# The pooling mixer as matrix products: group weights first, then band matrices, with the sums of the layer norm behind the last output tile

## The chip, the cores and the metric

The kernel runs on one core of a Trainium2 chip. A core has five engines that run side by side and are kept in step by semaphores: TensorE (PE in the profile, with its weight loads listed apart as PEld), VectorE (DVE), ScalarE (ACT), GpSimd (POOL) and SyncE (SP), which here only starts DMAs. The metric is the device time of one execution in microseconds; lower is better.

## What is computed

One inference step of a backbone with four layers, 1024 features and 384 tokens: a prompt of 128 and a sample of 256, which never mix. Each layer has a mixer and an MLP, and behind each of the two a residual and a layer norm. The mixers are, by layer: 0 an RG-LRU, 1 a short gated convolution, 2 a multi-scale pooling mixer, 3 an RG-LRU. The change concerns layer 2:

```python
WINDOWS = (2, 4, 8, 16)                       # one for each group of 256 features

def pool_mixer(x, w, scale):                  # x: tokens of one sequence
    S = cumsum of x over the tokens, with a zero in front
    for g, win in enumerate(WINDOWS):
        lo = clip(t - win // 2, 0, T)
        hi = clip(t + win - win // 2, 0, T)
        pooled[g] = (S[hi] - S[lo]) / (hi - lo)   # mean over a window, cut at the ends
    d = concat(pooled) - x
    y = d of group g times w[g]                   # 256 x 256 for each group
    return y * scale

x = layer_norm(ALPHA * x + g1 * out)
h = x * (1 + sc2) + sh2                       # the next input
```

Pooling works on the tokens alone and the group weights on the features alone, so the two can be done in either order.

## The kernel before

**Layout.** All activations lie transposed: eight tiles `Xt[c]` of 128 features (partitions) by 384 tokens (columns). A group of the pooling mixer is two tiles, `c = 2g` and `2g + 1`.

**Products in three parts.** Each float32 operand is split into a `hi` part, rounded to the type fp32r, and a `lo` part, the rest. A product is three TensorE instructions, hi·hi, lo·hi and hi·lo (`mm3`, lines 197 to 199 for the three). ScalarE writes the `hi` of weights (line 1289, `split_a`) and VectorE the `lo` (line 1295, `split_b`), 1024 columns at a time: half of a `raw` tile of 1 MB. The layer norm's sums are products with a matrix of 1/1024 (`ones_m`), in plain float32, which the profile lists as two records for each product.

**The order of the work.** `items` is a list of steps: `w` (half a weight tile, with a list of functions that are called one by one), `g` (a raw tile that is used as it is, mostly for the modulation vectors, `gemv`), `x` (a plain call) and `s` (a split). The loop at the end of the kernel runs through them. It calls `tick()` behind each function of a `w` item, and `defer(n, f)` runs `f` n ticks later. The splits of a weight half are deferred from three halves ahead (`LEAD`). Raw tiles have four buffers (`RAW_BUFS`) and are loaded by SyncE in the order of use as buffers come free (`issue`, line 1277). A scheduler then orders each engine's instructions: by the order of the program, but an instruction that is ready by its model may be put ahead of one that isn't. `tc.issue_after` holds instructions behind a given one on the same engine.

**Layer norm.** `ln_evac(idx)` gives a function `done(c, ps)` that adds an output tile to the residual (`resid`, line 547, two instructions, one for each sequence). From `c == 0` a mean over 128 features of the first tile is taken (`shift`, lines 567 and 568) and subtracted from all tiles (line 570). `stat(c)` squares a tile (line 582). Usually the sums over the tiles are kept on POOL or DVE (`s1t`, `s2t`, lines 594 to 598), and `stats_a` at the head of `ln_tail` makes four products of them (lines 619 to 622). With `late=True`, which only the pooling mixer uses, each tile and its square go to TensorE instead (line 588), one tile behind the outputs.

**The tail.** `tail` computes the variance `v` (line 648), its inverse root `r` (lines 649 to 655), and then, tile by tile in `chunk(c)`: subtract the mean (639), multiply by `r` (659), and `dst(c)`, the modulated `h` (705), its `hi` (718) and `lo` (723), and the next layer's `Xt[c]` (787 where the next norm is that of a mixer).

**The pooling mixer.** The tail ahead of it (`ln_tail(4, ..., lazy=True)`) leaves the tiles out; `pool_mix` calls `scaled(c)` and `pool_stage(c)` group by group from within the products (`before`). `lazy` also lets POOL subtract the mean for six tiles (line 647), and `kind == "pool"` lets ScalarE update `Xt[c]` (line 785). `pool_stage` works on DVE in a padded buffer of 392 or 408 columns: a shifted addition for windows 2 and 4 (lines 1113, 1116, 1117), a running sum and a difference for 8 and 16 (1119, 1122), a factor for the 8 columns at each end (1127), and the scaling and subtraction of `x` (1128). `new_h` then splits the result, with the `lo` part on POOL (line 723). Then come 16 products of 392 columns (`ORD_POOL`), two for each output tile.

**Around it.** `short_conv(1)` is layer 1's mixer; its first 32 weight tiles run with the input tiles outermost, so that TensorE can begin with the first tile of `h`. The tail ahead of it is `ln_tail(2, to_h(2, "mm"))`. `mlp(2)` follows the pooling mixer's own tail, `ln_tail(5)`.

## Time and profile before

| | |
|---|---|
| median of 3 runs | 1650.58 us (1650.07 to 1651.04) |
| profiled execution, its own time | 1649.62 us |
| its span, first to last instruction | 1647.8 us |
| mean granted TensorE clock | 0.989 |
| last product of layer 1's MLP starts | 881.29 us |
| variance (line 648) of the tail ahead of the pooling mixer | 884.36 us |
| first product of the pooling mixer | 898.68 us |
| variance (line 648) of the tail behind it | 931.80 us |
| first product of layer 2's MLP | 936.44 us |

Times inside the span are counted from its first instruction. A row of the timeline gives start, duration, engine, line, operation, output and inputs, and how many instructions of the kind were merged; a bracket gives the idle time ahead of it and what ended that. A row of the grouped lines gives the count, the total busy time and the mean in nanoseconds, and the idle time ahead of the group. A row of windows gives, for a stretch, its length, then the busy time and the number of instructions of PE, PEld, DVE, ACT and POOL, the granted clock, the busy share of the DMA engines and GB/s. TensorE instructions overlap, so their pace is read from one start to the next.

### The profile page before, as it was taken

The page shows a single profiled execution, that of the slowest core. Times are in us where ns is not written, and L with a number is a line of the kernel's source. Part 1 is how long each engine was busy: PE and PEld are TensorE (multiplying, and loading weights), DVE is VectorE, ACT ScalarE, POOL GpSimd, SP SyncE. Part 2 cuts the span into 40 slices and gives each one's busy share as a digit, 9 for nine tenths or more (in the row PEclk, how much of TensorE's full clock was granted, in tenths as well). Part 3 has the DMA queues.
Part 4 walks back from the last instruction along what each step waited for, and adds up shares of the span by engine and source line. Part 5 has one row for each costly group of instructions (what it writes and reads, how often), then busy time and mean ns, then how long its engine had stood idle before and what let it go on. Part 6 is the DMA issues. An engine that isn't in the chain of part 4 may idle for free.

```text
span 1647.8 us, 24431 instructions
## 1 busy us (share of the span) xinstructions
PE 1583.4 (96%) x9656; PEld 1501.8 (91%) x9656; DVE 1188.8 (72%) x1822; ACT 749.8 (46%) x1130; POOL 362.7 (22%) x445
## 2 busy tenths in 40 slices
PE   6999999999999999999997899999999999999996
PEld 5778899999999999999996599999988889999995
DVE  4789998886475569867746899688467997434544
ACT  3796642343253345324424553244259947423432
POOL 2114440002320146000055360000541134000043
PEclk9999999999999999999998999999999999999998
DMA  9677456556443535654543256546423344333321
GB/s 358 253 282 268 141 207 244 201 189 237 140 155 124 200 133 205 230 178 159 223 157 128 103 205 244 202 171 226 154 90 119 143 160 144 124 123 123 128 77 38
DMA packets 42162, 287.75 MB, mean 175 GB/s; under 512 B 4800, under 2 KB 6976, under 8 KB 8128
## 3 DMA queue, kind: packets, MB, share of 16 engines
q1 hardware_dynamic: 42048, 286.20, 48.4%
q8 instruction: 75, 1.23, 0.3%
q14 instruction: 39, 0.32, 0.1%
HBM read 284.59 MB, written 1.59 MB: 174 GB/s over the span
## 4 chain that ended last, share of the span: by engine, by line
PE 80%; DVE 12%; ACT 4%; issue 2%; POOL 1%; DMA 1%; SPq 0%; DVEq 0%; POOLq 0%; ACTq 0%
PE acc L197 26%; PE acc L199 25%; PE acc L198 25%; DVE wlo L1295 2%; DVE lru L879 1%; DMA raw<-in_wmod 1%; ACT hidf L930 1%; PE acc L453 1%; DVE X L570 1%; DVE hidf L958 1%; DVE X L547 1%; ACT L933 1%; ACT hidf L933 1%; DVE X L659 1%; POOL h L723 1%
## 5 line engine op out<-in xcount | busy, mean ns | idle before, releaser
L1295 DVE TENSOR_TENSOR wlo<-raw,whi 128x1024 fp32r<-128x1024 f32 x338 | 433.7, 1284 | 168.0 <-ACT whi L1289 166.7
L1289 ACT ACTIVATE whi<-raw 128x1024 fp32r<-128x1024 f32 x338 | 356.1, 1056 | 428.1 <-PE acc L199 351.7
L197 PE MATMUL acc<-h,whi 128*128 128x384 f32 (+2 forms) x1488 | 507.6, 341 | 16.0 <-ACT h L718 10.5
L198 PE MATMUL acc<-h,wlo 128*128 128x384 f32 (+2 forms) x1488 | 504.5, 339 | 0.0
L199 PE MATMUL acc<-h,whi 128*128 128x384 f32 (+2 forms) x1488 | 476.5, 340 | 3.1 <-POOL h L723 3.1
L197 PE MATMUL acc<-hid,whi 128*128 128x384 f32 (+1 forms) x1216 | 412.8, 340 | 0.8 <-ACT hid L975 0.8
L199 PE MATMUL acc<-hid,whi 128*128 128x384 f32 (+1 forms) x1216 | 409.4, 337 | 0.9 <-DVE hid L979 0.9
L198 PE MATMUL acc<-hid,wlo 128*128 128x384 f32 (+1 forms) x1216 | 409.2, 336 | 0.0
L197 PEld LDWEIGHTS acc<-h,whi 128*128 128x128 f32 x1488 | 280.9, 189 | 26.5 <-ACT h L718 11.6
L199 PEld LDWEIGHTS acc<-h,whi 128*128 128x128 f32 x1488 | 277.5, 188 | 6.7 <-POOL h L723 5.5
L198 PEld LDWEIGHTS acc<-h,wlo 128*128 128x128 f32 x1488 | 280.7, 189 | 1.6 <-issue 0.5
L197 PEld LDWEIGHTS acc<-hid,whi 128*128 128x128 f32 x1216 | 228.3, 188 | 5.2 <-issue 2.8
L199 PEld LDWEIGHTS acc<-hid,whi 128*128 128x128 f32 x1216 | 228.4, 188 | 1.5 <-DVE hid L979 1.5
L198 PEld LDWEIGHTS acc<-hid,wlo 128*128 128x128 f32 x1216 | 228.3, 188 | 0.9
L830 ACT ACTIVATE tmp<-acc,par 128x384 f32<-128x384 f32 x128 | 74.3, 580 | 259.1 <-PE acc L199 259.1
L570 POOL TENSOR_TENSOR X<-X,ssb 128x384 f32<-128x384 f32 x49 | 55.6, 1169 | 483.8 <-ACT ssb L568 483.8
L547 DVE SCALAR_TENSOR_TENSOR X<-acc,m,X 128x128 f32<-128x128 f32 (+1 forms) x176 | 64.7, 412 | 125.5 <-PE acc L199 123.7
L446 DVE SCALAR_TENSOR_TENSOR mac<-macr,sil,mac 128x512 f32<-128x512 f32 x176 | 126.2, 754 | 0.0
L832 DVE TENSOR_TENSOR tmp<-tmp 128x384 f32<-128x384 f32 x128 | 72.2, 564 | 65.8 <-ACT tmp L830 65.7
L446 DVE SCALAR_TENSOR_TENSOR mac<-mac,sil 128x512 f32<-128x512 f32 x132 | 95.2, 759 | 0.0
L777 POOL TENSOR_SCALAR X<-X,ag,xbb 128x128 f32<-128x128 f32 x64 | 94.8, 1495 | 0.4
L420 POOL TENSOR_SCALAR sc<-m 128x16 f32<-128x16 f32 x7 | 2.8, 403 | 328.6 <-DVE m L384 328.2
(194 smaller groups left out, 1310.6 us busy)
## 6 DMA issues: line engine op xcount, KB each, us to landing
raw<-in_w SPq DMA_DIRECT2D x128, 1024.0 KB, 4.8
raw<-in_wmodp SPq DMA_DIRECT2D x26, 1024.0 KB, 4.9
macr<-in_wmodv SPq DMA_DIRECT2D x22, 1024.0 KB, 5.3
mac<-in_wmodv SPq DMA_DIRECT2D x22, 1024.0 KB, 4.8
park<-in_wmodp SPq DMA_DIRECT2D x18, 1024.0 KB, 8.2
raw<-in_lin SPq DMA_DIRECT2D x16, 1024.0 KB, 5.1
raw<-in_scin SPq DMA_DIRECT2D x12, 1024.0 KB, 4.8
raw<-in_wmod SPq DMA_DIRECT2D x8, 1024.0 KB, 7.7
```

Source lines behind the costliest of these rows:

```text
L197: pe.matmul(ps, lhsT=hi, rhs=xhi, start=first, stop=False)
L198: pe.matmul(ps, lhsT=lo, rhs=xhi, start=False, stop=False)
L199: late = lambda: pe.matmul(ps, lhsT=hi, rhs=xlo, start=False, stop=last)
L446: vec.scalar_tensor_tensor(a, x, w, a, op0=ALU.mult, op1=ALU.add)
L547: vec.scalar_tensor_tensor(Xt[c][:, o : o + n], ps[:, a:b], col(g, c, k), Xt[c][:, o : o + n], op0=ALU.mult, op1=ALU.add)
L570: (vec if fast and i > 2 else gp).tensor_tensor(Xt[i], Xt[i], ssb, op=ALU.subtract)
L777: gp.tensor_scalar(Xt[c][:, a:b], Xt[c][:, a:b], col(g, c, k), col(xb, c, k), op0=ALU.mult, op1=ALU.add)
L830: act.activation(r, ps[:, :T], AF.Relu, bias=par_t[:, i : i + 1])
L832: vec.tensor_tensor(q, r, r, op=ALU.mult)
L933: act.activation(S["tau", c], S["tau", c], AF.Sqrt, scale=0.25)
L1289: act.activation(hi, raws[id(raw)][:, i * 1024 : (i + 1) * 1024], AF.Copy)
L1295: vec.tensor_tensor(lo, raws[id(raw)][:, i * 1024 : (i + 1) * 1024], hi.bitcast(F32), op=ALU.subtract)
```

## The change

The pooling is moved behind the group weights and onto TensorE. `first(g, k)` multiplies with the group weights, but the other way round: a 128-token slice of `h` is the stationary operand and 256 columns of weights move, so that the result `z` has tokens as partitions and features as columns. `z` for two groups fills one 512-column accumulator; there are three for each pair of groups, one for each 128 tokens (prompt, first and second half of the sample). Each is split into `hi` and `lo`. `second(c)` then makes output tile `c` by multiplying `z` with a band matrix that holds the window's weights minus one on the diagonal: 128 columns for the prompt, 256 for the first half of the sample and 136 for the second half. Products with columns where the band matrix is known to be zero are left out. The band matrices are an input (`band`), loaded and rounded ahead of layer 1's mixer by `band_load`; their rounding rest is kept only where it isn't zero (`finet`: the prompt's 128 columns and 8 columns at each end of the sample).

The tail ahead is now an ordinary one (`to_h(4, "mm")`, no `lazy`). With `late`, the first shift comes after 3 ticks instead of 5, DVE does all subtractions of it, `s1t` is summed on POOL, and the squares are kept in their tiles and all summed by products in `stats_a`, behind the last output tile.

```diff
-ORD_POOL = [(2 * g + k, 2 * g + m) for g in range(4) for m in range(2) for k in range(2)]
+ORD_POOL = [(2 * g + k, 2 * g + m) for g in range(4) for k in range(2) for m in range(2)]
+HALO = 8
+BAND = (P, TS, P + HALO)
+NBAND = sum(BAND)
+NFINE = P + 2 * HALO
...
         def done(c, ps):
             resid(c, ps, comb["g", idx], segs)
             if c == 0:
-                defer(5 if late else 3, shift)
+                defer(3, shift)
             elif 0 in sq:
+                if late:
+                    vec.tensor_tensor(Xt[c], Xt[c], ssb, op=ALU.subtract)
                 stat(c)
...
-            for i in range(6 if late else C):
-                (vec if fast and i > 2 else gp).tensor_tensor(Xt[i], Xt[i], ssb, op=ALU.subtract)
+            for i in [0] + held if late else range(C):
+                (vec if late or fast and i > 2 else gp).tensor_tensor(Xt[i], Xt[i], ssb, op=ALU.subtract)
             if late:
-                hcur["late"] = True
-                hcur["m"] = acc(), acc()
+                hcur["late"] = []
...
             act.activation(sq[c], Xt[c], AF.Square)
             if late:
-                lag = hcur.get("lag")
-
-                def sums():
-                    for m, x in zip(hcur["m"], (Xt[c], sq[c])):
-                        pe.matmul(m[:, :T], lhsT=ones_m, rhs=x, start=(c == 0), stop=(c == C - 1))
...
+                hcur["late"].append(sq[c])
+            if 0 < c < 7:
+                gp.tensor_tensor(s1t, Xt[0] if c == 1 else s1t, Xt[c], op=ALU.add)
+                if not late:
+                    s2eng.tensor_tensor(s2t, sq[0] if c == 1 else s2t, sq[c], op=ALU.add)
...
             m1, m2 = acc(), acc()
             hcur["m"] = (m1, m2)
+            many = hcur.pop("late", None)
+            if many:
+                for i, x in enumerate(many[:-1]):
+                    pe.matmul(m2[:, :T], lhsT=ones_m, rhs=x, start=i == 0, stop=False)
             pe.matmul(m1[:, :T], lhsT=ones_m, rhs=s1t, start=True, stop=False)
-            pe.matmul(m2[:, :T], lhsT=ones_m, rhs=s2t, start=True, stop=False)
+            if not many:
+                pe.matmul(m2[:, :T], lhsT=ones_m, rhs=s2t, start=True, stop=False)
...
-            on_pool = 2 if lazy or idx == 2 * DEPTH else C
+            on_pool = 2 if idx == 2 * DEPTH else C
...
-                if kind == "pool":
-                    act.activation(Xt[c], Xt[c], AF.Identity, bias=col(xb, c, 0), scale=col(g, c, 0))
-                else:
-                    gp.tensor_scalar(Xt[c], Xt[c], col(g, c, 0), col(xb, c, 0), op0=ALU.mult, op1=ALU.add)
+                gp.tensor_scalar(Xt[c], Xt[c], col(g, c, 0), col(xb, c, 0), op0=ALU.mult, op1=ALU.add)
...
+    def band_load(i):
+        n = 2 * NBAND
+
+        def f(raw):
+            two = lambda t, w: t.rearrange("p (g w) -> p g w", w=w)
+            src = two(raw[:, :n], NBAND)
+            hi = two(bandt[:, i * n : (i + 1) * n], NBAND)
+            lo = two(finet[:, i * 2 * NFINE : (i + 1) * 2 * NFINE], NFINE)
+            act.activation(hi, src, AF.Copy)
+            o = 0
+            for a, w in ((0, P), (BAND[0], HALO), (NBAND - HALO, HALO)):
+                x = slice(a, a + w)
+                vec.tensor_tensor(lo[:, :, o : o + w], src[:, :, x], hi[:, :, x].bitcast(F32), op=ALU.subtract)
+                o += w
+
+        G(band[i], f)
...
+        zps, z = {}, {}
+        done = ln_evac(2 * l, segs=((TS, T, 0), (0, TS, TP)), fast=True, late=True)
+
+        def first(g, k):
+            def f(hi, lo):
+                p, o = g // 2, g % 2 * 256
+                for t in range(3):
+                    if g % 2 == 0 and k == 0:
+                        zps[p, t] = acc()
+                    ps = zps[p, t][:, o : o + 256]
+                    xhi, xlo = (x[:, t * P : (t + 1) * P] for x in hcur[2 * g + k])
+                    pe.matmul(ps, lhsT=xhi, rhs=hi, start=k == 0, stop=False)
+                    pe.matmul(ps, lhsT=xhi, rhs=lo, start=False, stop=False)
+                    pe.matmul(ps, lhsT=xlo, rhs=hi, start=False, stop=k == 1)
+                if g % 2 == 1 and k == 1:
+                    for t in range(3):
+                        hi_, lo_ = (hidp.tile([P, 2 * LB], F32R, tag="hid", name=nm("z"))[:, :512] for _ in range(2))
+                        split_hi_lo(zps[p, t], hi_, lo_)
+                        z[p, t] = (hi_, lo_)
+                if g >= 2:
+                    for c in {(2, 1): (0,), (3, 0): (1,), (3, 1): range(2, C)}.get((g, k), ()):
+                        second(c)
+                        tick()
+
+            return f
+
+        def second(c):
+            g = c // 2
+            ps = acc()
+            f0 = c % 4 * P
+            w = lambda t, i: z[g // 2, t][i][:, f0 : f0 + P]
+            m = lambda i: bandt[:, g * NBAND + sum(BAND[:i]) : g * NBAND + sum(BAND[: i + 1])]
+            fine = finet[:, g * NFINE : (g + 1) * NFINE]
+            y, yp = ps[:, :TS], ps[:, TS:T]
+            left, right = y[:, : P + HALO], y[:, P - HALO :]
+            for n, (o, t, i, x) in enumerate(
+                (
+                    (yp, 0, 0, m(0)),
+                    (yp, 0, 0, fine[:, :P]),
+                    (yp, 0, 1, m(0)),
+                    (y, 1, 0, m(1)),
+                    (y[:, :HALO], 1, 0, fine[:, P : P + HALO]),
+                    (left, 1, 1, m(1)[:, : P + HALO]),
+                    (right, 2, 0, m(2)),
+                    (y[:, TS - HALO :], 2, 0, fine[:, P + HALO :]),
+                    (right, 2, 1, m(2)),
+                )
+            ):
+                pe.matmul(o, lhsT=w(t, i), rhs=x, start=n in (0, 3), stop=n in (2, 8))
+            done(c, ps)
+
+        raw = ["raw", poolw, 2]
+        for i in range(2):
+            items.append(("w", raw, i, [first(2 * i + g, k) for g in range(2) for k in range(2)]))
...
     ln_tail(2, to_h(2, "mm"), use)
+    band_load(0)
+    band_load(1)
     use = short_conv(1)
...
-    X(pool_alloc)
-    ln_tail(4, to_h(4, "pool"), use, lazy=True)
+    ln_tail(4, to_h(4, "mm"), use)
     pool_mix(2)
...
+            n = 1024 // len(it[3])
             for i, f in enumerate(it[3]):
-                s = slice(i * P, (i + 1) * P)
+                s = slice(i * n, (i + 1) * n)
```

On the order: each half of the group weights now has four functions, hence four ticks, instead of eight, and `second` adds a tick for each output tile. TensorE's program order in the second half is: `first(2,0)`, `first(2,1)`, tile 0, `first(3,0)`, tile 1, the product of `shift`, `first(3,1)`, tiles 2 to 7, then the ten products of the layer norm.

More of the change, by code (lines that the diff above doesn't have):

```diff
@@ L116 @@
     ("psc", C * 2),
-    ("pedge", 64),
 ):
@@ L130, in backbone_kernel @@
 @with_exitstack
-def backbone_kernel(ctx, tc, xT, par, wmod0, wmodp, wmodv, w1, w2, lin, lgate, lout, scin, scout, poolw, y_out, st_out):
+def backbone_kernel(ctx, tc, xT, par, wmod0, wmodp, wmodv, w1, w2, lin, lgate, lout, scin, scout, poolw, band, y_out, st_out):
     nc = tc.nc
@@ L1133, in pool_mix @@
-    def pool_mix(l):
-        todo = {}
-        def stage(g):
-            for c in (2 * g, 2 * g + 1):
-                todo[c] = hcur["scaled"](c)
-        def before(i):
-            if i % 4 == 0:
-                g = i // 4
-                if g == 0:
-                    stage(0)
-                if g < 3:
-                    stage(g + 1)
-                for c in (2 * g, 2 * g + 1):
-                    todo[c]()
-        linear(
-            [poolw],
-            ORD_POOL,
-            hrhs,
-            ln_evac(2 * l, segs=((0, TP, 0), (TP + 8, PG, TP)), fast=True, late=True),
-            2,
-            before=before,
-        )
+    bandt = const.tile([P, 4 * NBAND], F32R, tag="band", name="band")
@@ L1411, in _layout @@
     put("psc", _dup(_fm(a["pool_scale"][0])))
-    put("pedge", _pool_edges())
     r["par"] = par
```

129 lines of the change are left out of this document (34 added, 95 removed).

## The prediction

> **What bounds the kernel now.** I read the page first, then the windows around the pooling mixer, then its timeline, chain of waits and grouped lines.
>
> ```profile
> span 1647.8 us, 24431 instructions
> PE 1583.4 (96%) x9656; PEld 1501.8 (91%) x9656; DVE 1188.8 (72%) x1822; ACT 749.8 (46%) x1130; POOL 362.7 (22%) x445
> ...
> PE 80%; DVE 12%; ACT 4%; issue 2%; POOL 1%; DMA 1%; SPq 0%; DVEq 0%; POOLq 0%; ACTq 0%
> ```
>
> TensorE is busy for 96% of the span and makes 80% of the chain that ended last. So an edit that isn't in a gap of TensorE can win nothing. The pooling mixer is such a gap:
>
> ```profile
> 881.63:936.44 54.81, 36.31 (x219) 22.34 (x218) 47.16 (x89) 25.52 (x51) 26.53 (x21) 0.84 0.21 74
> ...
> 890.00:895.00 5.00, 0.00 (x0) 0.00 (x0) 5.00 (x10) 2.21 (x5) 3.02 (x4) 0.90 0.89 372
> 895.00:900.00 5.00, 1.02 (x2) 0.50 (x2) 5.00 (x14) 5.00 (x12) 1.29 (x1) 0.50 0.47 149
> ```
>
> Of the 54.8 us between the two MLPs TensorE is busy for 36.3, much of it at a lower clock (mean 0.84, and 0.50 once it has stood still), and DVE for 47.2. DVE sets the pace here. I measure the stage from one variance (line 648) to the next:
>
> ```profile
> 884.36 0.56 DVE L648 SCALAR_TENSOR_TENSOR tmp<-acc,tmp 128x384 f32<-128x384 f32 x1 [1.87 <-PE acc L622]
> ...
> 885.76 1.25 DVE L653 TENSOR_TENSOR tmp<-tmp,tmp 128x384 f32<-128x384 f32 x1
> ...
> 898.71 4.15 POOL L723 TENSOR_TENSOR h<-hidf,h 128x392 fp32r<-128x392 f32 x2 [4.43 <-ACT h L718]
> ...
> 931.80 0.56 DVE L648 SCALAR_TENSOR_TENSOR tmp<-acc,tmp 128x384 f32<-128x384 f32 x1 [1.88 <-PE acc L588]
> ```
>
> That is 931.80 - 884.36 = **47.4 us**, and what lies ahead of and behind it isn't touched. The chain of waits in it, by line, and the groups that the change removes:
>
> ```profile
> by line: POOL h L723 21.0%; PE acc L199 8.7%; issue 7.8%; DVE X L570 7.5%; DVE X L547 7.0%; PE acc L588 6.6%; DVE hidf L1122 4.9%; PE acc L198 4.6%; PE acc L197 4.6%; ACT h L718 3.6%; DVE X L672 3.5%; PE acc L567 3.2%; DVE wlo L1295 2.8%; D
> ```
>
> ```profile
> L723 POOL TENSOR_TENSOR h<-hidf,h 128x392 fp32r<-128x392 f32 x8 | 11.4, 1446 | 13.0 <-ACT h L718 13.0
> ...
> L1128 DVE SCALAR_TENSOR_TENSOR hidf<-hidf,hidf 128x392 f32<-128x392 f32 x8 | 5.1, 642 | 0.0
> ...
> L1119 DVE TENSOR_TENSOR_SCAN hidf<-hidf,hidf 128x408 f32<-128x408 f32 x4 | 4.6, 1183 | 0.0
> L1122 DVE TENSOR_TENSOR hidf<-hidf 128x392 f32<-128x392 f32 x4 | 4.4, 1130 | 0.0
> ...
> L1127 DVE TENSOR_TENSOR hidf<-hidf,par 128x16 f32<-128x16 f32 x16 | 3.5, 269 | 0.0
> ```
>
> POOL's `lo` parts (11.4 us busy) are the largest share of that chain, since TensorE waits for each, and the four DVE groups are 17.6 us.
>
> **The change, part by part.** *The tail ahead* becomes an ordinary one, and the trace holds such a tail, that of layer 1's mixer:
>
> ```profile
> 459.85 0.56 DVE L648 SCALAR_TENSOR_TENSOR tmp<-acc,tmp 128x384 f32<-128x384 f32 x1 [1.84 <-PE acc L622]
> ...
> 461.25 0.55 DVE L653 TENSOR_TENSOR tmp<-tmp,tmp 128x384 f32<-128x384 f32 x1
> ...
> 479.47 0.57 DVE L723 TENSOR_TENSOR h<-tmp,h 128x384 fp32r<-128x384 f32 x1
> ```
>
> ```profile
> L787 POOL TENSOR_SCALAR X<-X,ag,ab 128x384 f32<-128x384 f32 x8 | 8.6, 1080 | 17.1 <-ACT tmp L705 16.9
> L1295 DVE TENSOR_TENSOR wlo<-raw,whi 128x1024 fp32r<-128x1024 f32 x5 | 6.5, 1295 | 0.0
> ...
> L659 DVE TENSOR_TENSOR X<-X,tmp 128x384 f32<-128x384 f32 x8 | 4.3, 547 | 0.0
> L639 DVE TENSOR_TENSOR X<-X,acc 128x384 f32<-128x384 f32 x8 | 4.2, 543 | 0.0
> ```
>
> From the variance to the last `lo` it takes 480.04 - 459.85 = 20.2 us, with four weight splits of 1.3 us inside (the fifth starts at the end). The pooling mixer needs one of them in its tail: its halves are few, and the next split is deferred behind four ticks. So 20.2 - 3 x 1.3 = **16.3 us**. The six subtractions that POOL did and the eight `lo` parts are DVE's again, and are in that number. POOL's subtractions slowed DVE (line 653: 1.25 us against 0.55), and that goes too.
>
> *Behind it, on DVE.* Six `lo` parts of `z`, 512 columns: between 543 ns for 384 and 1295 for 1024 that is 0.69 us each, 4.2. Eight residuals, eight subtractions of the shift and the second split come on top:
>
> ```profile
> 929.17 0.74 DVE L547 SCALAR_TENSOR_TENSOR X<-acc,g,X 128x128 f32<-128x128 f32 x2 [0.39 <-PE acc L199]
> ```
>
> ```profile
> L570 DVE TENSOR_TENSOR X<-X,ssb 128x384 f32<-128x384 f32 x3 | 3.1, 1080 | 0.0
> ...
> L582 ACT ACTIVATE tmp<-X 128x384 f32<-128x384 f32 x9 | 4.7, 521 | 8.7 <-DVE X L547 6.9 <-POOL X L570 1.8
> ...
> L568 ACT ACTIVATE ssb<-acc 128x384 f32<-128x384 f32 x1 | 0.5, 494 | 1.4 <-PE acc L567 1.4
> ```
>
> The residuals are 8 x 0.74 = 5.9. A subtraction is 0.55 alone and 1.08 with POOL beside it; POOL now sums `s1t`, so I take 0.8, 6.4 in all (4.4 to 8.6). The split is 1.3. Together 4.2 + 5.9 + 6.4 + 1.3 = **17.8 us**. Behind the last subtraction come a square (0.52) and a product (0.81, below): 1.3.
>
> *TensorE's pace.* The trace has no fp32r product with fewer than 384 columns.
>
> ```profile
> 464.81 0.34 PE L198 MATMUL acc<-h,wlo 128*128 128x384 f32 x1
> 464.99 0.34 PE L197 MATMUL acc<-h,whi 128*128 128x384 f32 x1
> ...
> 902.39 0.53 PE L197 MATMUL acc<-h,whi 128*128 128x392 f32 x1
> 902.72 0.53 PE L198 MATMUL acc<-h,wlo 128*128 128x392 f32 x1
> ...
> 457.63 0.81 PE L620 MATMUL acc<-s2t,ones_m 128*128 128x384 f32 x2
> 458.28 0.81 PE L621 MATMUL acc<-X,ones_m 128*128 128x384 f32 x2
> ```
>
> From start to start 384 fp32r columns take 0.175 us at full clock (0.456 ns a column) and 0.33 at half; 384 float32 columns take 0.65 (1.69 ns). `first` is 72 products of 256 columns: 0.117 us each by columns, 0.175 if a load with a short product takes what one with a long product does. I take 0.117, nearest in form, so 1.05 us for each of the eight. An output tile is nine products with 1064 columns: 0.49 us by columns, 9 x 0.175 = 1.6 if none is shorter than the 384-column ones, and 808 x 1.69 + 256 x 0.456 ns = 1.5 if those under 256 columns go at the float32 price. I take **1.0**, the middle, as each has a load of its own.
>
> The `z` of groups 0 and 1 is ready at 16.3 + 3 x 0.69 = 18.4. Then TensorE's queue holds tile 0 (1.0), `first(3,0)` (1.05), tile 1 (1.0), the shift (0.65), `first(3,1)` (1.05): 4.75. The shift waits for DVE's residual of tile 0, and `first(3,1)`, all six further tiles and the norm stand behind it. The second `z` needs a copy of 512 columns (0.6, from 494 ns for 384) and 3 x 0.69, 2.7 in all, with tiles 2 and 3 beside it; then four tiles (4.0) and ten products (6.5). That ends at 18.4 + 4.75 + 2.7 + 4.0 + 6.5 = 36.4 us. DVE waits meanwhile for tile 0 (1.0) and for the shift and its copy (about 1.5): **2.5 us**. Its own sum is 16.3 + 17.8 + 2.5 + 1.3 = **37.9**, and it ends last. Queueing seven sums of squares behind the tiles costs TensorE 4.6 us that the old order had between products; DVE covers all but these 36.4, so I cost it at nothing, with 1.5 us of cover left.
>
> *The band loads* put two DMAs of 532 KB ahead of layer 1's weights in SP's queue, each holding one of four raw buffers, and two roundings of 1040 columns (1.07 us) on ACT and six small subtractions (about 0.6 us a load) on DVE into a stretch where both are full:
>
> ```profile
> 465.00:470.00 5.00, 5.00 (x30) 4.97 (x30) 5.00 (x10) 4.94 (x10) 2.11 (x4) 1.00 0.94 397
> ```
>
> ```profile
> 477.47 0.55 DVE L723 TENSOR_TENSOR h<-tmp,h 128x384 fp32r<-128x384 f32 x1
> ...
> 478.65 0.87 PE L199 MATMUL acc<-h,whi 128*128 128x384 f32 x4
> ```
>
> TensorE doesn't wait there, but has only 0.6 us to spare: 478.65 against 478.02. All in the way would be 3.4 - 0.6 = 2.8; behind the eight tiles of `h`, where splits are three halves ahead, it is nothing. I take 1.2.
>
> ```profile
> 463.38 1.19 SPq L1277 DMA_DIRECT2D raw<-in_scin  x2
> ```
>
> ```profile
> raw<-in_scin SPq DMA_DIRECT2D x12, 1024.0 KB, 4.8
> ```
>
> A load that moves behind a band's is issued at 464 and lands 4.8 us later, ahead of its split: nothing, at worst one landing, 4.8. A gain by these edits is excluded, since the old kernel has none of this work. The pool buffers' memsets go from POOL, off the chain, for nothing.
>
> *Sum.* 47.4 - 37.9 = 9.5 gained, 1.2 given back: 8.3. The profiled execution took 1649.62 us (span plus 1.8 around it), so 1641.3; it lies 0.96 under the median of 1650.58, so **1642** as a median. About 0.2% (3.3 us) can be told from no change.
>
> **The rivals.** *More* (0.17): the scheduler fills DVE's waits (2.5) with splits, the subtractions run at 0.55 (2.0) and the bands cost nothing: 33.4 us on DVE, and TensorE keeps up if a tile takes under 0.6: 1636.6. For it: DVE has 5.00 of 5.00 in the tail above. Against it: the long queue behind the shift.
>
> *The bands take it back* (0.11): 2.8 us on ACT and DVE and a late landing of 4.8: 7.6 lost of 9.5, 1648.7. For it: the margin of 0.6 us. Against it: the loads are ahead of need.
>
> *POOL stands in DVE's way* (0.06): each of POOL's 14 operations (eight updates, six sums) costs DVE the 0.7 us of line 653: 9.8, of which 2.0 is in my sum. The stage is 45.7 us, 1650.1. Against it: line 659 has 547 ns beside eight updates of line 787, which themselves take 1080. For it: line 653. [...]
>
> *Slower* (0.10), TensorE's queue: the clock stays at half, as in the window at 895, and narrow columns go at the float32 price. A tile is then 1.5 x 0.33 / 0.175 = 2.8 us. From 18.4: 2.8 + 2.0 + 2.8 + 1.2 + 2.0 = 10.8, two tiles 5.6, four tiles 11.2, the norm 6.5: 52.5 us, and with the bands' 1.2 it is 6.3 over: 1657. It decides from 2.0 us a tile on. The price alone doesn't do it: at full clock with 1.5 the queue ends at 39.5, 1644. For it: 0.50 when TensorE idles. Against it: TensorE now gets 1 us of work with each tile of `h`, every 2 us, and the row at 0.50 follows a window without any product. [...]
>
> **How the numbers follow.** The forecast has 0.56 (1638 to 1647 by itself: subtractions, waits and bands at their ends). Leaving out less than 2 in 10, the range runs from 1636, the better case, to 1651, past the two that come out even. Faster: 0.56 + 0.17 and a little of the bands' case, 0.78. Same 0.13, slower 0.09.
>
> **What would show it.** Variance to variance about 38 us instead of 47.4; the last `lo` of `h` 16 us behind the first variance; DVE busy nearly throughout; the nine products of a tile 1.0 us; tile 7's end ahead of DVE's last subtraction. It is wrong if TensorE waits in layer 1's first 16 us, if tiles take 2 us, or if the ten products of the norm run on long after DVE's last subtraction.

## The result, and the profile after

The changed kernel takes **1640.12 us** in the median (four executions, 1638.28 to 1640.46), the kernel before 1650.32 on the same chip: a ratio of 0.9937, with a 95% interval of 0.9925 to 0.9949. That is 10.2 us faster; 1642.0 was forecast, with a range of 1636 to 1651. The profiled execution took 1640.46 us with a span of 1638.7.

Line numbers have moved: the variance is line 642 now, the shift's subtractions 563 and 573, the residual 548, `first` 1102 to 1104, `second` 1139. The page's first rows, with busy time and share of the span, and its chain:

```profile
span 1638.7 us, 24573 instructions
PE 1585.4 (97%) x9740; PEld 1506.7 (92%) x9740; DVE 1180.6 (72%) x1817; ACT 748.5 (46%) x1128; POOL 344.0 (21%) x413
...
PE 79%; DVE 12%; ACT 5%; issue 2%; DMA 2%; POOL 1%; SPq 0%; DVEq 0%; POOLq 0%; ACTq 0%
```

TensorE is busy for 2 us more than before in a span that is 9.1 us shorter. From one variance to the next, the two profiled executions compare so (us, from the timeline's rows of the variance):

| stretch | before | after | difference |
|---|---|---|---|
| start to the variance ahead of layer 1's mixer, two stretches | 459.85 | 459.12 | -0.73 |
| layer 1's mixer (the bands are loaded here) | 142.92 | 144.11 | +1.19 |
| layer 1's MLP | 281.59 | 281.55 | -0.04 |
| the pooling mixer's stage | 47.44 | 35.46 | -11.98 |
| layer 2's MLP | 283.86 | 285.83 | +1.97 |
| layer 3's mixer | 140.64 | 140.56 | -0.08 |
| layer 3's MLP and the end | 291.50 | 292.07 | +0.57 |

So the stage gained 2.5 us more than forecast, the bands cost what was forecast, and a stretch that the change doesn't touch lost 2 us. The stage's timeline on DVE (start, duration, line, and in brackets the idle time ahead):

```profile
884.78 0.56 DVE L642 SCALAR_TENSOR_TENSOR tmp<-acc,tmp 128x384 f32<-128x384 f32 x1 [1.84 <-PE acc L616]
...
903.07 0.57 DVE L711 TENSOR_TENSOR h<-tmp,h 128x384 fp32r<-128x384 f32 x1
...
906.66 1.28 DVE L238 TENSOR_TENSOR z<-acc,z 128x512 fp32r<-128x512 f32 x2
907.85 1.02 DVE L573 TENSOR_TENSOR X<-X,ssb 128x384 f32<-128x384 f32 x2
908.78 0.74 DVE L548 SCALAR_TENSOR_TENSOR X<-acc,g,X 128x128 f32<-128x128 f32 x2
...
917.36 0.87 DVE L563 TENSOR_TENSOR X<-X,ssb 128x384 f32<-128x384 f32 x1
920.24 0.56 DVE L642 SCALAR_TENSOR_TENSOR tmp<-acc,tmp 128x384 f32<-128x384 f32 x1 [2.02 <-PE acc L616]
```

DVE hardly waits from 884.78 to 918.23, where its last subtraction ends: the only bracket in the whole listing between the two variances is one of 0.22 us, at 899.16 (a `lo` of `h` that waits for ScalarE). The `lo` parts of the second `z` (906.66) stand just where DVE would have waited for the shift's product and copy. The same stage by groups (busy us, mean ns; idle time ahead):

```profile
L548 DVE SCALAR_TENSOR_TENSOR X<-acc,g,X 128x128 f32<-128x128 f32 (+1 forms) x16 | 5.8, 406 | 0.0
L563 DVE TENSOR_TENSOR X<-X,ssb 128x384 f32<-128x384 f32 x6 | 5.2, 872 | 0.2
L653 DVE TENSOR_TENSOR X<-X,tmp 128x384 f32<-128x384 f32 x8 | 4.3, 548 | 0.0
...
L238 DVE TENSOR_TENSOR z<-acc,z 128x512 fp32r<-128x512 f32 x6 | 3.8, 679 | 0.0
...
L573 DVE TENSOR_TENSOR X<-X,ssb 128x384 f32<-128x384 f32 x2 | 1.0, 551 | 0.0
```

On TensorE the tiles follow each other at 1.01 us (the same product of two tiles in a row), and the norm's sums start 3.6 us ahead of DVE's last residual:

```profile
909.03 0.28 PE L1139 MATMUL acc<-fine,z 128*128 128x128 f32 x1
...
910.05 0.28 PE L1139 MATMUL acc<-fine,z 128*128 128x128 f32 x1
...
912.97 4.08 PE L611 MATMUL acc<-tmp,ones_m 128*128 128x384 f32 x12
917.28 0.91 PE L611 MATMUL acc<-tmp,ones_m 128*128 128x384 f32 x2 [0.23 <-ACT tmp L584]
918.03 0.81 PE L612 MATMUL acc<-s1t,ones_m 128*128 128x384 f32 x2
918.67 0.81 PE L615 MATMUL acc<-X,ones_m 128*128 128x384 f32 x2
919.32 0.81 PE L616 MATMUL acc<-tmp,ones_m 128*128 128x384 f32 x2
```

What TensorE did where the 1.97 us behind the stage were lost is in the windows there (length; busy us of PE, PEld, DVE, ACT, POOL; granted clock; DMA share; GB/s), cut where the clock changes:

```profile
922.59:926.00 3.41, 1.44 (x15) 1.21 (x8) 3.30 (x9) 1.74 (x4) 0.00 (x0) 1.00 0.92 348
926.00:929.42 3.42, 3.32 (x21) 1.54 (x20) 3.42 (x9) 3.36 (x7) 0.00 (x0) 0.50 0.96 378
929.42:932.83 3.41, 3.41 (x21) 3.41 (x21) 3.41 (x7) 3.41 (x8) 0.00 (x0) 1.00 0.96 336
```

TensorE stood still for 2 us until the first tile of `h`, and the clock was at half for the 3.41 us behind that. In the kernel before, it stayed at 1.00 in the same place, behind 1.98 us of work in the 3.42 from 935.00.

### The profile page after: what moved, and what is told of

Its sections match the earlier page's. It is cut to its first block, busy times and chain, and to the rows that moved or that the text cites. A ratio compares the mean times of both kernels' runs of the same rounds, so it can differ in the third digit from the quotient of the medians.

```text
span 1638.7 us, 24573 instructions
## 1 busy us (share of the span) xinstructions
PE 1585.4 (97%) x9740; PEld 1506.7 (92%) x9740; DVE 1180.6 (72%) x1817; ACT 748.5 (46%) x1128; POOL 344.0 (21%) x413
## 4 chain that ended last, share of the span: by engine, by line
PE 79%; DVE 12%; ACT 5%; issue 2%; DMA 2%; POOL 1%; SPq 0%; DVEq 0%; POOLq 0%; ACTq 0%
PE acc L198 25%; PE acc L199 25%; PE acc L200 25%; DVE wlo L1283 2%; DVE lru L858 1%; DMA raw<-in_wmod 1%; ACT hidf L909 1%; PE acc L454 1%; DVE X L548 1%; DVE hidf L937 1%; DVE X L653 1%; ACT L912 1%; ACT hidf L912 1%; DVE X L573 1%; DVE hidf L926 1%
## 5 line engine op out<-in xcount | busy, mean ns | idle before, releaser
L198 PE MATMUL acc<-h,whi 128*128 128x384 f32 (+2 forms) x1472 | 499.8, 340 | 7.1 <-DVE h L688 6.6
L199 PE MATMUL acc<-h,wlo 128*128 128x384 f32 (+2 forms) x1472 | 498.2, 338 | 0.0
L200 PE MATMUL acc<-h,whi 128*128 128x384 f32 (+2 forms) x1472 | 469.0, 339 | 0.0
L198 PEld LDWEIGHTS acc<-h,whi 128*128 128x128 f32 x1472 | 277.0, 188 | 16.3 <-issue 11.4
L199 PEld LDWEIGHTS acc<-h,wlo 128*128 128x128 f32 x1472 | 276.9, 188 | 1.0 <-issue 0.2
L200 PEld LDWEIGHTS acc<-h,whi 128*128 128x128 f32 x1472 | 274.1, 188 | 1.3 <-DVE X L633 0.8
L573 POOL TENSOR_TENSOR X<-X,ssb 128x384 f32<-128x384 f32 x46 | 52.0, 1165 | 483.1 <-ACT ssb L571 483.1
L761 POOL TENSOR_SCALAR X<-X,ag,xbb 128x128 f32<-128x128 f32 x64 | 89.8, 1418 | 0.4
```

What stands on the lines that cost most here:

```text
L198: pe.matmul(ps, lhsT=hi, rhs=xhi, start=first, stop=False)
L199: pe.matmul(ps, lhsT=lo, rhs=xhi, start=False, stop=False)
L200: late = lambda: pe.matmul(ps, lhsT=hi, rhs=xlo, start=False, stop=last)
L573: (vec if late or fast and i > 2 else gp).tensor_tensor(Xt[i], Xt[i], ssb, op=ALU.subtract)
L761: gp.tensor_scalar(Xt[c][:, a:b], Xt[c][:, a:b], col(g, c, k), col(xb, c, k), op0=ALU.mult, op1=ALU.add)
```

## The experiments

Each is the changed kernel with one edit, or the kernel before with one. The ratio is always to the kernel before, run beside it on the same chip. "Stage" is variance to variance in the profiled execution.

| run | median us | ratio, interval | stage us |
|---|---|---|---|
| the change | 1640.1 | 0.9937 [0.9925, 0.9949] | 35.46 |
| bands_later | 1638.0 | 0.9929 [0.9916, 0.9943] | 35.50 |
| sums_between | 1647.4 | 0.9981 [0.9972, 0.9990] | 41.22 |
| tiles_twice | 1646.7 | 0.9978 [0.9969, 0.9987] | 42.34 |
| gemv_mid | 1639.9 | 0.9940 [0.9928, 0.9953] | 36.31 |
| sq_lag1 | 1654.9 | 1.0032 [1.0018, 1.0046] | 47.73 |
| sq_lag2 | 1642.2 | 0.9963 [0.9946, 0.9979] | 36.14 |
| before_lo_dve | 1649.1 | 0.9993 [0.9984, 1.0003] | 46.82 |
| before_tail | 1657.3 | 1.0043 [1.0028, 1.0058] | 53.46 |
| lag1_fill | 1644.4 | 0.9967 [0.9955, 0.9979] | 39.53 |
| fill | 1641.4 | 0.9950 [0.9936, 0.9963] | 35.46 |
| bands_fill | 1637.2 | 0.9926 [0.9913, 0.9938] | 35.46 |
| before_fill | 1652.3 | 1.0017 [1.0008, 1.0026] | 48.20 |

### The band loads elsewhere

In the changed kernel's trace the second band's rounding stands on ScalarE ahead of the inverse root of the norm (line 643), and DVE waits for that:

```profile
459.90 1.07 ACT L1081 ACTIVATE band<-raw 128x1040 fp32r<-128x1040 f32 x1 [0.95 <-DMA raw<-in_band]
460.88 0.51 ACT L643 ACTIVATE tmp<-tmp 128x384 f32<-128x384 f32 x1
```

The edit moves both loads into the middle of layer 1's MLP:

```diff
-    band_load(0)
-    band_load(1)
     use = short_conv(1)
...
     use = mlp(1, ORD_MOD_DVE[1])
+    for i in range(2):
+        band_load(i)
+        items.insert(len(items) - 41 + 10 * i, items.pop())
```

> The two band loads are moved from the place ahead of layer 1's mixer into the middle of layer 1's MLP, where TensorE has 12 us of split weights in hand. Theory: in the changed kernel they cost 1.2 us, because the rounding of the second band (1.07 us on ACT) runs between the square of the mean and the inverse root of layer 1's tail; then variance to variance from layer 1's first tail to its second falls from 144.1 to 142.9 us and the time from 1640.1 to 1638.9. Rival: the cost comes from the raw buffers or the transfers, and moves with them: no change, 1640.

The same row of ScalarE, with the variance at 458.79 in this execution:

```profile
459.44 0.53 ACT L643 ACTIVATE tmp<-tmp 128x384 f32<-128x384 f32 x1 [0.82 <-DVE tmp L642]
```

The inverse root comes 0.65 us behind the variance and not 1.76, and layer 1's mixer is back at 142.91 us from 144.11; layer 1's MLP keeps its 281.53, with the same two loads in it. So the price doesn't move with the loads. These rows of the changed kernel's DVE show the rest of it:

```profile
461.49 0.56 DVE L647 TENSOR_TENSOR tmp<-tmp,tmp 128x384 f32<-128x384 f32 x1 [0.89 <-ACT tmp L643]
461.96 0.42 DVE L1085 TENSOR_TENSOR fine<-raw,band 128x256 fp32r<-128x256 f32 x1
...
462.76 0.26 DVE L1085 TENSOR_TENSOR fine<-raw,band 128x16 fp32r<-128x16 f32 x2
```

From the variance to DVE's step behind the inverse root (line 647) it takes 2.37 us here and 1.40 with the later loads, 0.97 less; to the first tile's product with `r` (line 653) 4.43 and 3.24, 1.19 less. So 0.97 us of the price is the one rounding, and 0.22 the bands' small subtractions between the next steps of the norm. The time, 1638.0 us (1638.9 expected), can't be told from the 1640.1 of the change: the intervals overlap.

### The sums between the tiles again

Each tile and its square go to TensorE again, one tile behind, as the kernel before does; the pooling stays on TensorE, and POOL's sum is left out.

```diff
...
-                hcur["late"].append(sq[c])
-            if 0 < c < 7:
+                lag = hcur.get("lag")
+                def sums():
+                    for m, x in zip(hcur["m"], (Xt[c], sq[c])):
+                        pe.matmul(m[:, :T], lhsT=ones_m, rhs=x, start=(c == 0), stop=(c == C - 1))
+                hcur["lag"] = sums
+                if lag:
+                    lag()
+            elif 0 < c < 7:
...
```

> The pooling by products stays, but the layer norm's sums are put back between the output tiles, a tile and its square as products with one tile lag, and POOL's sums are left out. Theory: DVE sets the pace behind the tiles and TensorE is 3.6 us ahead at tile 7, so the order on TensorE has no price; DVE's subtractions go from 0.87 to 0.55 us without POOL beside them (six times 0.3) and two products instead of four follow the last square (1.3 less): the stage from variance to variance falls from 35.5 to 32 or 33 us, 1637 to 1638. Rival: that all tiles are queued ahead of the sums is what won the time; then each tile waits behind the sums of the one before, the stage is longer by 3 us or more, 1643 or more.

My theory fell here: the stage is 5.8 us longer. Each of DVE's residuals waits for TensorE, in steps of 2.30 us, with DVE busy for 1.3 of them:

```profile
913.89 0.74 DVE L548 SCALAR_TENSOR_TENSOR X<-acc,g,X 128x128 f32<-128x128 f32 x2 [0.97 <-PE acc L1151]
914.66 0.56 DVE L563 TENSOR_TENSOR X<-X,ssb 128x384 f32<-128x384 f32 x1
916.19 0.74 DVE L548 SCALAR_TENSOR_TENSOR X<-acc,g,X 128x128 f32<-128x128 f32 x2 [0.97 <-PE acc L1151]
```

2.30 is a tile (1.01) and two float32 products (0.65 each): TensorE's work of a step is over DVE's. The subtraction takes 0.56 us without POOL's sum beside it, and 0.87 with it. But the steps could as well be a chain of waits, so the next runs separate the two.

### Each tile twice

```diff
-            for n, (o, t, i, x) in enumerate(
+            for n, (o, t, i, x) in 2 * list(enumerate(
...
-            ):
+            )):
```

> Each output tile's nine products are issued twice, the second time over the first, so that a tile costs TensorE 2.0 us instead of 1.0; the output is the same. Theory: at 1.0 us TensorE is 3.6 us ahead of DVE's 1.6 us a tile, and at 2.0 it becomes the bound: the last tile ends about 8 us later and the norm's products follow, so the stage grows by 6 to 8 us, 1646 to 1648. Rival: DVE has so much to do that tiles are free: at most 1 us more, 1641.

As expected: the stage is 42.34 us, 6.9 more, and a step is 2.02 us. TensorE has about a third of a step to spare in the changed kernel (1.01 us of work in DVE's 1.56). What is over that goes to the time, 0.46 us in each of six steps, 2.8 in all, but that is less than half of the 6.9. At the end TensorE now finishes the last tile just as DVE comes to it, so the seven queued sums of squares have nothing left to stand behind: the variance waits 5.24 us behind DVE's last subtraction and not 2.02, which is 3.2 more. The cover for these sums is gone, and it was worth about as much as the steps.

### One sum of squares between the tiles

Only the square goes to TensorE between the tiles, one tile behind (sq_lag1) or two (sq_lag2); POOL keeps `s1t`.

```diff
...
-                hcur["late"].append(sq[c])
+                q = hcur["late"]
+                q.append(lambda: pe.matmul(hcur["m2"][:, :T], lhsT=ones_m, rhs=sq[c], start=(c == 0), stop=(c == C - 1)))
+                if len(q) > 1:
+                    q.pop(0)()
...
```

> The new kernel with the sums of squares as products between the output tiles again, each one tile behind; the pooled sum s1t stays on POOL, so TensorE has one float32 product (0.65 us) in each step and not two. What made the two sums of the run before cost 5.8 us is either their number or their place. If number (TensorE had 2.30 us of work in a step against 1.6 of DVE): a step is now 1.01 + 0.65 = 1.66 us on TensorE against 1.6 on DVE, the stage is 35.5 to 36.5 us, the time 1639 to 1641. If place (the product of tile c's square stands ahead of tile c + 2, and the square comes only behind the residual and the subtraction): residual 0.73, subtraction 0.87, square 0.6, product 0.65 and tile 1.01 follow each other over two steps, 2.0 us a step, and the stage is 37.5 to 38.5 us, the time 1642 to 1643. Behind the last subtraction only three or four products are left in each case.

> As the run with one tile of lag, with two: the product of a square then stands ahead of the third tile behind its own, and the chain of 4.0 us is spread over three steps, 1.3 us, under DVE's 1.6. By place: the loss of the run beside it is gone, the stage is 35.5 to 36 us. By number: the same 35.5 to 36.5 for both. If the stage is longer than 37 us here too, neither is right, and a float32 product between tiles costs something of its own.

With two tiles of lag the expectation holds: 36.14 us. Two of its executions, without a trace, took 1650.25 and 1652.07 us, though, at a mean clock of 0.988 and 0.987, where six took 1640.7 to 1642.5 at 0.993 to 0.995; whether that is the fall of the clock shown below stays open. With one, **both** of its cases fell: 47.73 us, and the kernel is slower than the one before. The row of TensorE's first square, and the windows around it, cut at 3.41 us, show why:

```profile
909.32 0.91 PE L588 MATMUL acc<-tmp,ones_m 128*128 128x384 f32 x2 [1.89 <-ACT tmp L585]
```

```profile
906.77:910.18 3.41, 1.52 (x6) 0.64 (x6) 2.40 (x5) 1.49 (x3) 0.86 (x1) 1.00 0.23 96
910.18:913.59 3.41, 3.41 (x15) 2.80 (x14) 1.30 (x3) 0.21 (x1) 0.24 (x2) 0.50 0.00 0
...
927.25:930.66 3.41, 3.41 (x9) 1.73 (x9) 1.30 (x3) 0.52 (x1) 0.04 (x1) 0.50 0.00 0
930.66:934.07 3.41, 3.41 (x34) 1.67 (x38) 1.26 (x3) 1.02 (x2) 0.00 (x0) 1.00 0.02 5
```

The wait of 1.89 us leaves TensorE 1.52 us of work in 3.41. Then the granted clock is 0.50 for 20.5 us, six such stretches, though TensorE is busy in all of them. A step takes 3.20 us, all of it TensorE's:

```profile
924.81 0.74 DVE L548 SCALAR_TENSOR_TENSOR X<-acc,g,X 128x128 f32<-128x128 f32 x2 [1.86 <-PE acc L1146]
...
928.01 0.74 DVE L548 SCALAR_TENSOR_TENSOR X<-acc,g,X 128x128 f32<-128x128 f32 x2 [1.86 <-PE acc L1146]
```

### The same order with the wait filled

To see whether the clock or the order costs the 11.6 us between the two lags, two products that nobody reads go into that wait:

```diff
             sq[0] = True
+            if late:
+                idle = acc()
+                for _ in range(2):
+                    pe.matmul(idle[:, :T], lhsT=ones_m, rhs=ssb, start=True, stop=True)
             stat(0)
```

> The run with the squares' sums one tile behind, whose granted clock fell to 0.50 at 910.18 and stayed there for 20.5 us, with one edit: behind the shift's product stand two float32 products that nobody reads (1.3 us), which wait for the shift's copy, so that they fill TensorE's wait for the first square (1.89 us there). Nothing else moves, and no work goes. Theory (the 12 us that this order cost over the one with two tiles of lag are the clock: at half clock a step is 3.20 us of TensorE, at full clock it isn't TensorE that sets it): the clock is 1.00 throughout the stage, the steps are 1.7 to 2.0 us, the stage 36 to 38.5 us, the time 1640.5 to 1643. Rival (the order itself, a product that stands ahead of the next tile and waits for ScalarE): the stage stays over 45 us, the time over 1650, whatever the clock is.

```profile
905.01:908.42 3.41, 2.32 (x7) 1.04 (x7) 3.21 (x8) 1.73 (x4) 0.06 (x1) 1.00 0.48 204
908.42:911.83 3.41, 3.41 (x23) 2.79 (x22) 1.30 (x3) 0.54 (x2) 1.02 (x2) 1.00 0.00 0
```

With 1.3 us of work added the stage is **8.2 us shorter**, 39.53 against 47.73, and the kernel 10.5 us faster: the clock is 1.00 through the whole stage. It is 1.0 us over the range that I gave. Against two tiles of lag 3.39 us are left: 2.14 ahead of tile 2, where the filling itself stands, 0.61 in the five steps behind it (1.88 us each in the mean, against 1.75), and 0.64 at the end. So one float32 product a step costs little in either place, and what made sq_lag1 slower than the kernel before was the clock. With two products a step (sums_between) the clock was 1.00 and it was TensorE's work.

### Where the gain in the stage came from

Two edits to the kernel before: POOL's `lo` parts on DVE, and the ordinary tail with everything else kept.

```diff
-        new_h(c, s[:, :PG], PG, lo_eng=gp)()
+        new_h(c, s[:, :PG], PG)()
```

> The kernel before with one edit: the lo parts of the pooled tiles on DVE and not on POOL. In the chain of its stage the largest share is POOL's lo, 21%, but DVE is busy for 45 of the stage's 47.4 us. Theory (DVE's work bounds the old stage, the chain through POOL only fills its gaps): eight lo parts of 0.56 us come to DVE, 4.5 us, and what POOL's reads cost it (1.13 us for a difference, 0.70 for the product with the inverse root, against 0.55) goes, 3 to 4 us: stage 46 to 50 us, time 1648 to 1653. Rival (the eight waits for POOL's lo are what the change gained): stage 38 to 42 us, time 1641 to 1645.

```diff
-        new_h(c, s[:, :PG], PG, lo_eng=gp)()
+        return new_h(c, s[:, :PG], PG, lo_eng=gp)()
...
-            for i in range(6 if late else C):
+            for i in range(C):
...
-            before=before,
...
-    ln_tail(4, to_h(4, "pool"), use, lazy=True)
+    ln_tail(4, to_h(4, "pool"), use)
```

> The kernel before with the ordinary tail and nothing else: all tiles are centred, scaled and pooled one after the other in the tail, DVE subtracts the mean, and the pooling stays on DVE with POOL's lo. Theory (the gain is DVE's pooling of 17.6 us that went): DVE gets six subtractions of the mean and two of the shift more (4.4 us), less what POOL cost it: stage 45 to 50 us, time 1648 to 1653. Rival (the held tail was the loss): stage under 43 us, time under 1646.

The `lo` parts held the largest share of the old chain, 21%, and moving them changes nothing that can be told: 46.82 us of stage against 47.44. These are the stage's totals of the kernel before, of before_lo_dve and of the changed kernel, one window each (columns as above):

```profile
884.36:931.80 47.44, 30.97 (x166) 19.72 (x162) 41.97 (x77) 22.01 (x45) 26.53 (x21) 0.82 0.19 68
```

```profile
883.31:930.13 46.82, 32.90 (x184) 20.34 (x180) 41.13 (x85) 22.18 (x45) 15.33 (x13) 0.82 0.22 80
```

```profile
884.78:920.24 35.46, 31.64 (x250) 24.05 (x246) 32.75 (x66) 21.12 (x43) 14.21 (x16) 1.00 0.25 90
```

Eight `lo` parts (5.1 us) came to DVE in the second, and it is busy for 0.8 us less: with POOL at work for 15.3 us instead of 26.5, other instructions of DVE are shorter (the factors of line 1127 take 2.0 us and not 3.5, the differences of line 1122 2.9 and not 4.4). In the changed kernel DVE has 9.2 us less work, and that is most of the 12.0; the other 2.8 is idle time of DVE, 5.5 us before and 2.7 after.

The tail by itself is a **loss** of 6.0 us, more than I expected (53.46 against 45 to 50). Its windows:

```profile
881.76:901.76 20.00, 11.21 (x98) 7.52 (x90) 19.86 (x40) 14.11 (x27) 5.72 (x4) 0.80 0.28 107
901.76:919.00 17.24, 3.24 (x5) 1.51 (x6) 17.24 (x35) 6.05 (x12) 8.44 (x9) 0.50 0.14 44
919.00:935.22 16.22, 16.22 (x65) 11.40 (x67) 5.47 (x13) 3.99 (x9) 0.87 (x1) 0.94 0.05 20
```

First DVE pools everything (busy for 37.1 of 37.2 us, TensorE for 14.5), then TensorE does everything (16.2 of 16.2, DVE 5.5). The held tail had woven the two together. The ordinary tail pays only once pooling is no work of DVE's.

### The stretch behind the stage

First the late group of modulation products is moved ahead, in between the halves of the pooling weights, and the tail behind keeps three:

```diff
+            if i == 1:
+                GV(1)
             items.append(("w", raw, i, [first(2 * i + g, k) for g in range(2) for k in range(2)]))
...
-    ln_tail(5, to_h(5, "mm"), ng=4)
+    ln_tail(5, to_h(5, "mm"), ng=3)
```

> One of the four modulation chunks of the tail behind the pooling mixer is used between the two halves of the group weights instead, so that three chunks are left, all loaded by then. Theory: of the 2.0 us that the changed kernel loses between that tail's variance and the next MLP's tail, 1.5 come from the fourth chunk, which waits for its load and holds TensorE's queue while the clock falls to 0.5: the first lo products start 7.2 us behind the variance instead of 8.5, and the time goes from 1640.1 to 1638.6. Rival: the clock falls because TensorE stands still for 2 us behind the third chunk in any case: at most 0.4 us is won. Against both: the chunk between the halves may hold up the group products, at most 1 us.

It gives back 0.85 us in the stage and wins 1.41 behind it, though the clock falls there as before, to 0.50 from 926.27 to 929.69: the late group's products, 1.93 us at half clock in the changed kernel's trace (from 926.83), are no longer in that stretch. In the time, gemv_mid can't be told from the change. Then two products that nobody reads go into TensorE's 2.0 us of standstill, behind the modulation's:

```diff
             act.activation(y0, v, AF.Abs_reciprocal_sqrt)
+            if idx == 5:
+                idle = acc()
+                for _ in range(2):
+                    pe.matmul(idle[:, :T], lhsT=ones_m, rhs=msq, start=True, stop=True)
```

> The new kernel with two float32 products that nobody reads (1.3 us) behind the modulation's products at the head of the tail behind the pooling mixer, where TensorE stands still for 2.0 us until the first tile of h; they end 0.6 us ahead of it. Theory (the 1.97 us that layer 2's MLP takes longer are mostly the granted clock, 0.50 from 926.00 to 929.42, which follows a stretch of 3.41 us with TensorE 42% busy): that stretch is 80% busy, the clock stays at 1.00, the modulation's fourth group of products takes 1.1 us and not 1.9, and the MLP's interval is 284.1 to 285.0 us and not 285.8; the time is 1638.3 to 1639.3. Rival (the 1.97 us are the late landing of that group's weights, 926.78, which the clock doesn't change): the interval stays at 285.5 to 286.2, the time at 1640.

```profile
922.59:926.00 3.41, 2.93 (x23) 1.55 (x16) 3.27 (x8) 1.16 (x3) 0.00 (x0) 1.00 0.89 310
926.00:929.42 3.42, 2.88 (x28) 1.98 (x27) 3.42 (x9) 3.36 (x7) 0.00 (x0) 1.00 0.93 371
1340.55:1343.97 3.42, 1.48 (x7) 0.92 (x6) 3.21 (x6) 0.53 (x1) 2.57 (x2) 1.00 0.26 110
1343.97:1347.38 3.41, 3.41 (x7) 1.69 (x5) 0.30 (x1) 1.01 (x2) 0.00 (x0) 0.50 0.02 5
```

The clock holds, and layer 2's MLP takes 284.81 us and not 285.83, as the theory had it. The time doesn't follow: 1641.4 us, where 1638.3 to 1639.3 was expected. In the profiled execution the clock falls at another place instead, at the end of layer 3's mixer, which takes 142.26 us and not 140.56: 1.70 us, half of a stretch of 3.41. The other executions have no trace, so whether that is what kept the median up stays open.

The profiled executions of all the runs say more about this stretch than the filling does. Wherever the clock fell at the head of layer 2's MLP, with the late group in its place, the MLP took 285.74 to 286.22 us: the change, bands_later, sq_lag1, sq_lag2, lag1_fill, and before_fill, which is the old kernel. Wherever it held, the MLP took 283.30 to 284.81: the old kernel, before_lo_dve, before_tail, sums_between, tiles_twice, fill and bands_fill. In tiles_twice and sums_between the code of this stretch is the changed kernel's and TensorE stands still for 1.97 and 2.05 us as it does there, and yet the clock holds, at 284.20 and 284.27 us. So the fall costs about 1.6 us here, and it isn't tied to the change.

Both mends together:

> The two edits that each mend one loss of the new kernel, together: the band loads in the middle of layer 1's MLP, and the two products that keep TensorE busy behind the pooling mixer. If the losses are independent: 1640.1 - 1.2 (bands) - 1.2 (clock) = 1637.7, 1636.5 to 1638.5. Rival (in the run with the later bands alone the weights of the modulation's fourth group were late too, by 0.66 us, and the landing sets the head of the MLP): no more than the bands bring, 1638 to 1639.

```profile
920.62:924.03 3.41, 2.93 (x29) 1.40 (x22) 3.27 (x8) 0.91 (x2) 0.00 (x0) 1.00 0.82 259
```

1637.2 us, the lowest median of all, as expected from independent losses: layer 1's mixer is at 142.92, layer 2's MLP at 284.28, layer 3's mixer at 140.58. In this trace and in that of bands_later the clock is at 0.50 for one stretch of 3.41 us inside the stage (from 896.7 and from 896.2), and the stage takes 35.46 and 35.50 us all the same: in that part TensorE doesn't set the pace. The interval of this run overlaps those of the change and of the later bands alone, so the runs don't tell it apart from either for certain; against the kernel before it is 0.7% faster.

### The clock in the kernel before

Fourteen products that nobody reads stand where the old kernel's TensorE was idle, behind the modulation's:

```diff
             act.activation(y0, v, AF.Abs_reciprocal_sqrt)
+            if lazy:
+                idle = acc()
+                for i in range(14):
+                    pe.matmul(idle[:, :T], lhsT=ones_m, rhs=ssb if i else msq, start=i == 0, stop=i == 13)
```

> The kernel before with 14 float32 products that nobody reads (9.1 us) behind the modulation's products, where TensorE stands still from 887.5 to 898.7 and the granted clock then is 0.50 until 907.70. They end 2 us ahead of the first pooled tile. Theory (DVE's work sets the old stage, so the half clock costs it next to nothing): the clock is 1.00 where it was 0.50, and the stage is 46.5 to 47.5 us, the time 1649.5 to 1650.5. Rival (a part of the 12 us that the change won in the stage is TensorE's clock): the stage is 42 to 45 us, the time 1645 to 1648.

```profile
892.92:896.34 3.42, 3.42 (x12) 1.91 (x11) 3.42 (x10) 3.42 (x8) 0.25 (x1) 1.00 0.13 53
896.34:899.75 3.41, 1.06 (x4) 0.30 (x2) 3.41 (x9) 3.41 (x9) 2.15 (x1) 1.00 0.83 310
899.75:903.16 3.41, 2.37 (x7) 2.18 (x8) 3.41 (x8) 1.92 (x5) 2.17 (x3) 0.50 0.00 0
```

This one settles nothing: the clock held while the filling ran and fell at 899.75, as the pooled tiles' first products came with waits for POOL between them. The stage is 48.20 us, no shorter. How much of the old stage was the clock's stays open; if DVE's own work doesn't depend on that clock, it can be no more than the 2.8 us of idle time that DVE lost.

## Why the prediction was right, point by point

**The stage was bound by DVE, and it is DVE's work that went.** Right: DVE is busy for 9.2 us less in it, neither half of the old structure (the tail, POOL's `lo`) gives the gain alone, and a clock of 0.50 for 3.41 us of the stage (bands_later, bands_fill) doesn't lengthen it. No run puts work back on DVE alone, so that 9.2 us of the gain are DVE's rests on the traces' busy times. The rival "POOL stands in DVE's way" is small: a subtraction takes 0.87 us beside POOL's sum and 0.55 without, 1.9 us more for six, and all eight take 6.2 where I had 6.4.

**The terms.** Right in size where they are operations: residuals 5.8 us (5.9 forecast), subtractions 5.2 + 1.0 (6.4), the `lo` parts of `z` 679 ns (690), a tile 1.01 us (1.0). The last `lo` of `h` comes 18.9 us behind the variance, not 16.3, because work of the second part is already in it (a `lo` of `z`, two transposes, a second split); that is nearly all work moved, not added. The mis-sized term is **DVE's waits: 2.5 us forecast, 0.2 measured**. I had put the wait for tile 0 and that for the shift in series with everything, but the `lo` parts of the second `z` fill both. The case *More* named this mechanism, with splits for the filling. The end is the other way: 2.0 us behind the last subtraction and not 1.3, since the product of the last square stands behind those of `s1t` and of the last tile. Together: 2.3 of waits and 0.9 that is left for the smaller terms, less 0.7 at the end, make 2.5, the difference between 37.9 and 35.46.

**The cover of the queued sums.** Costing them at nothing was right for this order: TensorE was done with the tiles 3.6 us before DVE began on the last of them. The reason was thinner than it looked, since one sum a step between the tiles is also nearly free when it lags by two tiles (36.14), and two a step cost 5.8 us. It does rest on the cover: with tiles at 2.0 us (tiles_twice) the sums cost 3.2 us at the end.

**The bands.** Right in size (1.19 us, 1.2 forecast), wrong in place, so the size was luck. I had looked at the head of layer 1's mixer, at splits and tiles of `h` with 0.6 us to spare. TensorE has no wait among them, but it waits for the first tile of `h`, 1.56 us where it was 0.38, and those 1.18 us are the price. The prediction named a wait of TensorE there as a sign of being wrong; it came, as large as the term. The rounding landed a few microseconds earlier than I had looked, ahead of the inverse root, where one instruction of ScalarE is on the path by itself.

**"What lies ahead of and behind it isn't touched."** This step failed, by 1.97 us in the profiled pair: the head of layer 2's MLP ran at half clock for 3.41 us. The step left out that a stretch with the same code has two lengths, with such a fall (285.74 to 286.22 us) and without (283.30 to 284.81); the change's trace had it and that of the kernel before didn't. That the old kernel has it too, in before_fill, makes the 1.97 more likely chance, by where the grid of the clock fell, than a price of the change. With the filling 1.02 of it goes; there TensorE then waits 0.54 us for the late group's load. What the prediction held against the slower case, that the row at 0.50 follows a window without any product, didn't carry: stretches with 1.44 us of work in 3.41 (here) and 1.52 (sq_lag1) were followed by 0.50.

**The slower rival** was dearer than its 0.10 in one respect: sq_lag1 is that case, with TensorE at half clock and a step of 3.20 us, and one product queued at a different place was enough for it. Its threshold was too high: the case was to decide from 2.0 us a tile on, but DVE's step is 1.56 us, and at 2.02 (tiles_twice) the stage has already grown by 6.9. Nor was its price for narrow columns paid: at full clock a product of 128 columns takes 0.12 us from start to start (909.03 to 909.15 in the changed kernel's trace), where 128 x 1.69 ns would be 0.22.

## What to carry to other kernels

When an engine's work is taken off a path, what was woven around it can go too, but not ahead of it: the plain tail costs 6 us as long as the pooling is on DVE. Price a small instruction by the one that stands behind it in its queue, not by how full the engine is. And before queueing a TensorE instruction that waits for another engine, look at how much work is left to TensorE around it: in sq_lag1 it was 1.52 us in 3.41, the clock was 0.50 for the 20.5 us behind that, and the stage took 47.73 us, where two filling products made it 39.53 and a place one tile later in the queue 36.14.

## What the runs showed of the hardware

The granted clock changed on a grid of 3.41 us in these traces: in the kernel before it fell at 894.04, rose at 907.70, fell at 917.94 and rose at 921.35, which is four steps, three and one; in sq_lag1 it fell at 910.18 and rose at 930.66, six steps apart. Around the stage and at the end of layer 3's mixer it fell behind stretches of 3.41 us with 0.62 us of TensorE's work (gemv_mid, from 922.86), 1.34 (the kernel before, from 914.52), 1.44 (the change, from 922.59) and 1.54 (before_tail, from 1354.55), and once behind one with 2.04 (before_fill, from 916.81); it held behind one with 1.98 (the kernel before, from 935.00) and one with 1.57 (the same trace, from 1351.43). The share alone doesn't decide it, then: of these two stretches of the kernel before the first has 1.45 us of work, 28 products with a stationary operand of 32 columns, and the clock held until the empty one behind it was over.

```profile
887.22:890.63 3.41, 1.45 (x28) 0.62 (x20) 3.38 (x3) 0.00 (x0) 3.41 (x4) 1.00 0.54 151
890.63:894.04 3.41, 0.00 (x0) 0.00 (x0) 3.41 (x8) 1.25 (x3) 2.16 (x3) 1.00 1.01 425
```

Nor did a stretch with TensorE busy throughout always bring the clock back: five in a row didn't in sq_lag1, with narrow products (128, 8, 136 columns) between the float32 ones, and the sixth, mostly float32, did. What decides it isn't shown by any run.

One such fall came with 1.2 to 2.1 us more in layer 3's mixer, which no run touches: it took 140.56 to 140.64 us in the eight traces (of fourteen) without a fall there, and 141.83 to 142.61 in the six with one; the head of layer 2's MLP behaves alike, as shown above. Differences of 2 us between these kernels can be that alone.

Beside POOL, DVE's instructions took longer in one place and not in another. DVE's subtraction took 0.56 us in sums_between, without POOL's sum of two tiles, and 0.87 in the changed kernel beside it, where the sum itself took 1.00, while the changed kernel's product with the inverse root (line 653) stayed at 0.548 with POOL's update of a tile beside it. The two differ in POOL's work, but also in which came first: the sum was under way (from 909.01 us) when the subtraction started (909.56), while the products at 896.06 and 897.93 had started ahead of the updates (896.10, 898.33), and there it was the updates that grew, from 0.66 to 1.04 and 1.06. No run separates the two.
